# One more down-projection unit ahead of the next block's output projection, in a Hymba-style encoder layer on one core

## The chip, the core and the metric

The kernel runs on one core of a Trainium2 chip. The time is device microseconds of one execution, the median of three runs. The engines named here are TensorE (PE: matmuls and transposes, PEld its weight loads), VectorE (DVE), ScalarE (ACT), GpSimd (POOL) and SyncE (SP), whose queue issues the loads from and stores to device memory.

## The reference

One layer over 2048 tokens of width 1024, in float32, and then a final norm:

```python
h = rmsnorm(x, norm1_g)
proj = h @ w_in                       # q, k, v, z, xbc, dt
attn = rmsnorm(windowed_attention(q, k, v, sink, cos, sin), attn_out_g)
ssd = ssd_mixer(z, silu(dwconv(xbc)), dt, ...)   # two scans, gated, normed
mixed = concatenate([attn, ssd])
x = x + mixed @ w_out
h = rmsnorm(x, norm2_g)
u = dwconv(h @ w_up, ffn_conv_w, ffn_conv_b)     # 3 taps, 2 x 2816 columns
gate, val = split(u, 2)
x = x + (silu(gate) * val) @ w_down
return rmsnorm(x, final_norm_g)
```

## The kernel before

Activations lie with channels on the partitions. The 2048 tokens make four blocks of 512 (`NB`), and block `j` has `x1_j` (8 tiles of 128 channels by 512 tokens) as its residual stream, named `x` in the trace.

**Matmuls in three products.** Each float32 operand is split into a rounded high part and a low part. `mm3` (L105 to L108) makes hi times hi (L106), hi weight times lo activation (L107) and lo weight times hi activation (L108), all three into the same PSUM tile.

**Weights.** `wplan` lists every weight slice in the order of its use. `w_raw` loads a slice into `wraw` (L127, SP queue), `w_split` makes its high part `whi` on ScalarE (L141) and its low part `wlo` mostly on GpSimd (L142). `next_w` hands out the next slice and starts those behind it. `wraw`, `whi` and `wlo` have two buffers each, so slice n + 2 is cast when slice n is used up. A slice of `w_out` or `w_up` has 1024 columns (512 KB), one of `w_down` for a group of three pairs has 768 (384 KB).

**The feed-forward part of a block.** The 22 channel pairs (gate and value) come in six groups: 4, 4, 4, 4, 3, 3. For each pair `up_mm` makes two PSUM tiles of 24 matmuls and `up_unit` does convolution and gate (`fa`, `fth`) and writes `f` and its low part. `down_unit(j, g, cp)` adds group `g` to two tiles of `x1`: two PSUM tiles (`dn_b`), for a group of three pairs 9 matmuls each, and after each an update of `x` on VectorE (L1108). The units of group `g - 1` follow the up pairs of group `g`.

**The PSUM tiles** of up, `wo` and `dn` come from one pool, `psm`, with four buffers; each unit takes two.

**Between the blocks.** Beside block `j` run attention and scan of block `j + 1` (the `side` streams), which fill `mx`, named `mixed`. When they are done, `wo_split` scales `mx` and splits it into `m_hi` (ScalarE, L989) and `m_lo` (VectorE, L990), 8 tiles in two calls of 4. `wo_x1` loads the new residual `x1_{j+1}` (L996, 2 MB); `wo_unit` (four of them, 48 matmuls each) multiplies by `w_out`, adds to `x1_{j+1}` (L1029) and adds the square to `n_ss`. `h2_stage` has two steps. The first, `rstd_cols`, transposes the sum of squares on TensorE (`r_ps`), reduces it, and takes the power on GpSimd. The second, `rstd_bcast` and the loop behind it, transposes the result back (`r_pr`), copies it (`r`), and makes the 8 tiles `h2t` (L1040, VectorE) with `h_hi` (L207, ScalarE) and `h_lo` (L208, VectorE and GpSimd in turn). The first up pair of block `j + 1` reads them; for this pair the products go over the 8 tiles with both weights at each tile.

**Order.** The program order of a unit of work is that of the calls. The kernel is built with `tile.TileContext(nc, schedule_with_timeline_sim=True)`: a planner with modelled times sets the order on each engine, and may place a later instruction ahead of one that it takes to be waiting. Buffers of a pool are handed out by it too.

Of the kernel before, what the change touches and what calls it, by code (L numbers as in the profile page):

```python
# [28 lines left out]
GROUPS = [(0, 4), (4, 4), (8, 4), (12, 4), (16, 3), (19, 3)]  # L29
# [28 lines left out]
def block_kernel(ctx: ExitStack, tc: tile.TileContext, a: dict, out: bass.AP):  # L58
# [46 lines left out]
    def mm3(ps, whi, wlo, xhi, xlo, first, last):  # L105
        nc.tensor.matmul(ps, whi, xhi, start=first, stop=False)  # L106
        nc.tensor.matmul(ps, whi, xlo, start=False, stop=False)  # L107
        nc.tensor.matmul(ps, wlo, xhi, start=False, stop=last)  # L108
# [6 lines left out]
    wplan = [(a["w_ch"][c], 1024) for c in range(2)]  # L115
# [3 lines left out]
    def w_raw(i):  # L119
        if i >= len(wplan) or i in wraws:  # L120
            return
        src, m = wplan[i]
        raw = wpool.tile([P, 1024], F32, tag="wraw", name="wraw")
        dst = raw[:, :m]
        if len(src.shape) == 3:
            dst = dst.rearrange("p (i n) -> p i n", i=2)
        nc.sync.dma_start(dst, src)  # L127
        wraws[i] = raw

    def w_split(i):  # L130
        if i >= len(wplan) or i in wdone:
            return
        w_raw(i)
        m = wplan[i][1]
        raw = wraws[i]
        if i in wplace:
            hi, lo = wplace.pop(i)
        else:
            hi = wpool.tile([P, 1024], F32R, tag="whi", name="whi")
            lo = wpool.tile([P, 1024], F32R, tag="wlo", name="wlo")  # L140
        A.copy(hi[:, :m], raw[:, :m])  # L141
        (V if i < WV or i in WVS else G).tensor_tensor(lo[:, :m], raw[:, :m], hi[:, :m].bitcast(F32), ALU.subtract)  # L142
        wdone[i] = (hi, lo)

    def next_w():
        i = wpos[0]
        wpos[0] += 1
        w_split(i)
        w_raw(i + 1)
        w_split(i + 1)  # L150
        w_raw(i + 2)
        return wdone.pop(i)
# [35 lines left out]
    def new_ss(name):  # L188
        return [tpool.tile([P, FW], F32, tag="rstd", name=f"{name}_ss", bufs=1)]
# [98 lines left out]
    def flush():  # L288
        for f in pend:
            f()  # L290
        pend.clear()
# [25 lines left out]
    def new_mm(name):  # L317
        return [psm.tile([P, 512], F32, tag="mm", name=f"{name}_b{b}") for b in range(2)]
# [727 lines left out]
    def up_mm(j, pr, ws):  # L1046
        h2hi, h2lo = h2[j]
        ps = new_mm(f"up{j}_{pr}")
        if len(ws) > 2:
            ps += new_mm(f"up{j}_{pr + 1}")  # L1050
        order = [(i, k) for k in range(NK) for i in range(len(ws))]
        for i, k in order if pr == 0 else sorted(order):
            mm3(ps[i], ws[i][0][:, ksl(k)], ws[i][1][:, ksl(k)], h2hi[:, k], h2lo[:, k], k == 0, k == NK - 1)
        return ps
# [42 lines left out]
    def down_unit(j, g, cp, fs, w):  # L1097
        k0, nk = GROUPS[g]
        whi, wlo = w
        x1 = xone[j]  # L1100
        if j < NB - 1:
            ps = new_mm(f"dn{j}_{g}_{cp}")
            for i in range(2):
                for k in range(nk):
                    kk = ksl(i * nk + k)
                    mm3(ps[i], whi[:, kk], wlo[:, kk], fs[:, k, 0, :TB], fs[:, k, 1, :TB], k == 0, k == nk - 1)
                xv = x1[:, 2 * cp + i, 0:TB]
                V.tensor_tensor(xv, xv, ps[i], ALU.add)  # L1108
            return
        for i in range(2):  # L1110
            for b in range(2):
                down_part(j, g, 2 * cp + i, b, fs, w)
# [3 lines left out]
    def down_part(j, g, c, b, fs, w):  # L1116
        k0, nk = GROUPS[g]
        x1 = xone[j]
        n0, n1 = PART[b]
        pool, tag = (pss, "sc") if c % 2 == 0 else (psa, "ac")  # L1120
        ps = pool.tile([P, 512], F32, tag=tag, name=f"dn{j}_{g}_{c}_{b}")
        for k in range(nk):
            q = (c % 2) * nk + k
            mm3(
                ps[:, : n1 - n0], w[0][:, ksl(q)], w[1][:, ksl(q)],
                fs[:, k, 0, n0:n1], fs[:, k, 1, n0:n1], k == 0, k == nk - 1,
            )
        n1 = min(n1, TB + 1)
        V.tensor_tensor(x1[:, c, n0:n1], x1[:, c, n0:n1], ps[:, : n1 - n0], ALU.add)
# [82 lines left out]
    def w_wo():  # L1212
        return [(a["w_out"][c], 1024) for c in range(NK)]

    def w_dn(g):
        k0, nk = GROUPS[g]
        return [(a["w_dn"][cp][:, :, k0 * P : (k0 + nk) * P], 2 * nk * P) for cp in range(4)]
# [17 lines left out]
    for j in range(NB):  # L1235
        for g, (k0, nk) in enumerate(GROUPS):
            wplan += [(a["w_up"][k0 + i, q], 1024) for i in range(nk) for q in range(2)]
            if g > 0:
                wplan += w_dn(g - 1)
        if j + 1 < NB:  # L1240
            wplan[-2:-2] = w_wo()
        wplan += w_dn(len(GROUPS) - 1)

    def step(streams, n=1):
        for _ in range(n):
            for s in streams:
                next(s, None)

    def drain(s):
        for _ in s:  # L1250
            pass
# [105 lines left out]
    def start_side(j):  # L1357
        side.clear()
        due[:] = [0.0, 0.0]
        if j == NB:  # L1360
            return None
        m = new_mixed(j)
        side.extend([(chunks(attn, j, m), RATE[0]), (chunks(ssd, j, m), RATE[1])])
        return m

    def pace(n):
        for i, (s_, rate) in enumerate(side):
            due[i] += n * rate
            while due[i] >= 1:
                due[i] -= 1  # L1370
                next(s_, None)
# [12 lines left out]
    for j in range(NB):  # L1384
        more = j + 1 < NB
        if j > 0:
            mx = start_side(j + 1)
        fss = []
        for g, (k0, nk) in enumerate(GROUPS):
            fs = big.tile([P, SLOT], F32R, tag="big", name=f"f{j}_{g}").rearrange(  # L1390
                "p (k s n) -> p k s n", k=4, s=2
            )
            i = 0
            if j == 0 and g == 0 and UP2:
                wt = big.tile([P, SLOT], F32R, tag="big", name="wup")
                for q in range(2):
                    wplace[wpos[0] + 2 + q] = [wt[:, 1024 * (2 * q + z) : 1024 * (2 * q + z) + 1024] for z in range(2)]
                ps = up_mm(j, 0, [next_w() for _ in range(4)])
                for i in range(2):
                    if RPD == i:  # L1400
                        drain(rp)
                    up_unit(j, i, fs, i, ps[2 * i : 2 * i + 2])
                    pace(2)
                i = 2
            for i in range(i, nk):
                drain(rp)
                up_unit(j, k0 + i, fs, i, up_mm(j, k0 + i, [next_w(), next_w()]))
                step([fin], 2)
                pace(2)
            fss.append(fs)  # L1410
            if g == len(GROUPS) - 1:
                flush()
                for s_, _ in side:
                    drain(s_)
            if not more and g == len(GROUPS) - 1:
                wt = [big.tile([P, SLOT], F32R, tag="big", name=f"wdn{z}") for z in range(2)]
                for q in range(4):
                    wplace[len(wplan) - 4 + q] = [t[:, 768 * q : 768 * q + 768] for t in wt]
            if g > 0:
                for cp in range(4):  # L1420
                    if more and g == len(GROUPS) - 1 and cp == 2:
                        break
                    down_unit(j, g - 1, cp, fss[g - 1], next_w())
                    pace(1)
                    if more and g == len(GROUPS) - 1:
                        wo_split(j + 1, mx, 4 * cp, 4 * cp + 4)
        g = len(GROUPS) - 1
        if more:
            wo_x1(j + 1)
            ss = new_ss(f"n2_{j + 1}")  # L1430
            for cp in range(4):
                wo_unit(j + 1, cp, [next_w(), next_w()], ss)
            h2s = h2_stage(j + 1, ss)
            for cp in (2, 3):
                down_unit(j, g - 1, cp, fss[g - 1], next_w())
                step([h2s])
        else:
            last_down(g, fss[g])
            return
        for cp in range(4):  # L1440
            down_unit(j, g, cp, fss[g], next_w())
            step([h2s])
        fin = final(j)
# [79 lines left out]
```

## Time and profile before

| | |
|---|---|
| median of 3 runs | 2461.11 us |
| lowest, highest | 2459.13, 2463.56 us |
| profiled execution: its time | 2459.2 us |
| profiled execution: span from first to last instruction | 2457.1 us |
| busy TensorE, VectorE, ScalarE, GpSimd | 96%, 69%, 44%, 44% of the span |
| mean granted TensorE clock | 0.987 of full speed |

In a row of a timeline the first number is the start in us from the start of the span, the second the duration in us, then engine, line, operation, output and inputs with shapes. `x4` means that four like instructions are merged into the row. What stands in brackets is the idle time of that engine just before the row, and what ended it. Where a row says `<-DVE x L1108`, the instruction started when line 1108 on VectorE, which writes `x`, was done.

### The profile page before, as it was taken

Reading aid. Unit: us, or ns where it says so; the run is one execution under the profiler, and the core shown is the slowest. Engines: PE = TensorE matmul, PEld = TensorE weight load, DVE = VectorE, ACT = ScalarE, POOL = GpSimd, SP = SyncE. Lnnn points to the kernel's source line nnn. Section 1 sums busy time; section 2 is a strip of 40 time slices with the busy share of each in tenths; the row PEclk is TensorE's granted clock in tenths of the full one; section 3 lists DMA queues with packets and bytes.
Section 4 is the critical chain, followed back from the end, with each engine's and each line's share of the span. In section 5 each row is a group of like instructions: output and inputs, shape, how many; then the busy total and the mean of one; then the engine's idle time right before and its main releaser. Section 6 shows DMA issues by size and latency. Waiting matters only on the chain.

```text
span 2457.1 us, 31337 instructions
## 1 busy us (share of the span) xinstructions
PE 2347.2 (96%) x11440; PEld 1955.7 (80%) x11440; DVE 1687.5 (69%) x3056; ACT 1075.5 (44%) x1818; POOL 1086.0 (44%) x585
## 2 busy tenths in 40 slices
PE   8999999897999999999999999999999999999997
PEld 6878797776788878778787877787888877788887
DVE  5757777777886684569877675698776556844445
ACT  5444656345454443435443443354444333433334
POOL 1114314463644544455444454555444436544444
PEclk9999999998999999999999999999999999999999
DMA  6567445883444333334434333343342232333332
GB/s 229 166 194 221 134 148 181 253 274 115 130 129 126 117 125 101 124 93 152 123 117 128 122 112 116 92 153 118 114 129 90 86 121 85 121 103 95 95 92 80
DMA packets 172461, 325.82 MB, mean 133 GB/s; under 512 B 12690, under 2 KB 83730, under 8 KB 172308
## 3 DMA queue, kind: packets, MB, share of 16 engines
q1 hardware_dynamic: 172308, 323.83, 41.8%
q8 instruction: 90, 1.47, 0.2%
q14 instruction: 63, 0.52, 0.1%
HBM read 277.77 MB, written 44.71 MB: 131 GB/s over the span
## 4 chain that ended last, share of the span: by engine, by line
PE 45%; DVE 14%; POOL 2%; ACT 2%; issue 2%; DMA 1%; DVEq 0%; POOLq 0%; ACTq 0%
PE up_b L108 8%; PE up_b L107 8%; PE up_b L106 8%; DVE fa L1065 4%; PE dn_b L106 3%; PE dn_b L107 3%; PE dn_b L108 3%; PE dn L107 2%; PE dn L106 2%; PE dn L108 2%; PE wo_b L108 2%; PE wo_b L106 2%; PE wo_b L107 2%; POOL wlo L142 1%; DVE ab L893 1%
## 5 line engine op out<-in xcount | busy, mean ns | idle before, releaser
L142 POOL TENSOR_TENSOR wlo<-wraw,whi 128x1024 fp32r<-128x1024 f32 (+1 forms) x306 | 738.2, 2413 | 895.4 <-ACT whi L141 837.6
L108 PE MATMUL up_b<-h_hi,wlo 128*128 128x512 f32 x1392 | 551.7, 396 | 14.7 <-POOL wlo L142 14.7
L106 PE MATMUL up_b<-h_hi,whi 128*128 128x512 f32 x1392 | 551.3, 397 | 3.4 <-ACT whi L141 2.3
L107 PE MATMUL up_b<-h_lo,whi 128*128 128x512 f32 x1392 | 549.2, 395 | 1.9 <-DVE h_lo L208 1.9
L141 ACT CAST whi<-wraw 128x1024 fp32r<-128x1024 f32 (+1 forms) x330 | 338.9, 1027 | 467.6 <-PE up_b L107 120.9
L1065 DVE SCALAR_TENSOR_TENSOR fa<-up_b,fcw,fa 128x511 f32<-128x511 f32 (+2 forms) x396 | 271.7, 687 | 211.2 <-ACT fa L1067 206.7
L108 PEld LDWEIGHTS up_b<-h_hi,wlo 128*128 128x128 f32 x1392 | 262.4, 189 | 77.7 <-POOL wlo L142 21.1
L106 PEld LDWEIGHTS up_b<-h_hi,whi 128*128 128x128 f32 x1392 | 261.9, 188 | 62.7 <-ACT whi L141 4.9
L107 PEld LDWEIGHTS up_b<-h_lo,whi 128*128 128x128 f32 x1392 | 262.1, 188 | 60.0 <-DVE h_lo L208 3.4
L106 PE MATMUL dn_b<-f,whi 128*128 128x512 f32 x528 | 211.4, 400 | 0.4 <-DVE x L1108 0.2
L107 PE MATMUL dn_b<-f,whi 128*128 128x512 f32 x528 | 208.7, 395 | 0.0
L108 PE MATMUL dn_b<-f,wlo 128*128 128x512 f32 x528 | 204.2, 397 | 0.0
L1092 ACT CAST f<-fth 128x512 fp32r<-128x512 f32 (+1 forms) x88 | 54.6, 620 | 216.5 <-DVE fth L1089 175.5
L1087 ACT ACTIVATE fth<-fa 128x512 f32<-128x512 f32 (+1 forms) x88 | 55.6, 632 | 212.6 <-DVE fa L1065 167.6
L1108 DVE TENSOR_TENSOR x<-x,dn_b 128x512 f32<-128x512 f32 x144 | 97.6, 681 | 59.9 <-PE dn_b L108 59.6
L1067 ACT ACTIVATE fa<-up_b,fcw 128x512 f32<-128x512 f32 x176 | 135.9, 773 | 0.2
L106 PEld LDWEIGHTS dn_b<-f,whi 128*128 128x128 f32 x528 | 99.8, 189 | 22.9 <-DVE x L1108 1.1
L108 PEld LDWEIGHTS dn_b<-f,wlo 128*128 128x128 f32 x528 | 99.3, 188 | 22.5 <-POOL wlo L142 0.2
L107 PEld LDWEIGHTS dn_b<-f,whi 128*128 128x128 f32 x528 | 99.2, 188 | 21.0
L893 DVE SCALAR_TENSOR_TENSOR ab<-ab,ldt,mask 128x128 f32<-128x128 f32 x256 | 95.3, 442 | 21.8 <-DMA ab<-acs_d 21.8
L1065 DVE SCALAR_TENSOR_TENSOR fa<-hal,fcw,fa 128x2 f32<-128x2 f32 (+1 forms) x264 | 101.0, 383 | 4.6
L1093 DVE TENSOR_TENSOR f<-fth,f 128x512 fp32r<-128x512 f32 (+1 forms) x88 | 78.9, 897 | 30.9 <-ACT f L1092 30.1
(333 smaller groups left out, 4880.4 us busy)
## 6 DMA issues: line engine op xcount, KB each, us to landing
wraw<-in_w_up SPq DMA_DIRECT2D x176, 512.0 KB
wraw<-in_w_dn SPq DMA_DIRECT2D x64, 512.0 KB
wraw<-in_w_out SPq DMA_DIRECT2D x36, 512.0 KB
ab<-acs_d SPq DMA_DIRECT2D x32, 512.0 KB
wraw<-in_w_ch SPq DMA_DIRECT2D x28, 512.0 KB
wraw<-in_w_dn SPq DMA_DIRECT2D x32, 384.0 KB
ak<-ks_d SPq DMA_DIRECT2D x14, 768.0 KB
xt<-in_x SPq DMA_DIRECT2D x16, 512.0 KB
```

The lines of the kernel that those rows point to most:

```text
L106: nc.tensor.matmul(ps, whi, xhi, start=first, stop=False)
L107: nc.tensor.matmul(ps, whi, xlo, start=False, stop=False)
L108: nc.tensor.matmul(ps, wlo, xhi, start=False, stop=last)
L141: A.copy(hi[:, :m], raw[:, :m])
L142: (V if i < WV or i in WVS else G).tensor_tensor(lo[:, :m], raw[:, :m], hi[:, :m].bitcast(F32), ALU.subtract)
L893: (G if i < SUBP[0 if first else 1] else V).scalar_tensor_tensor(ab[:, i, d], ab[:, i, d], ldt[:, d, c, h : h + 1], mask3[:, 2 * d * P : ( ...
L1065: V.scalar_tensor_tensor(o, src, w(q), o, ALU.mult, ALU.add)
L1067: A.activation(ai[:, 0:TB], u, AF.Identity, bias=w(3), scale=w(2))
L1087: A.activation(th[:, :n], acc[:, 0, :n], AF.Tanh)
L1092: A.copy(fs[:, idx, 0, :n], th[:, :n])
L1093: V.tensor_tensor(fs[:, idx, 1, :n], th[:, :n], fs[:, idx, 0, :n].bitcast(F32), ALU.subtract)
L1108: V.tensor_tensor(xv, xv, ps[i], ALU.add)
```

## The change

Group 4 is the last but one. Its four down units stood two ahead of the next block's output projection and two behind it; now three stand ahead and one behind. The weight order follows: the eight slices of `w_out` go in ahead of the last slice of group 4 in place of the last two. The two calls of `wo_split` stay behind the first and the second unit. Behind the output projection the first step of `h2_stage` now comes at once, then the last unit of group 4, then the second step. The last block is as it was.

```diff
         if j + 1 < NB:
-            wplan[-2:-2] = w_wo()
+            wplan[-1:-1] = w_wo()
         wplan += w_dn(len(GROUPS) - 1)
...
                 for cp in range(4):
-                    if more and g == len(GROUPS) - 1 and cp == 2:
+                    if more and g == len(GROUPS) - 1 and cp == 3:
                         break
                     down_unit(j, g - 1, cp, fss[g - 1], next_w())
                     pace(1)
-                    if more and g == len(GROUPS) - 1:
+                    if more and g == len(GROUPS) - 1 and cp < 2:
                         wo_split(j + 1, mx, 4 * cp, 4 * cp + 4)
...
             h2s = h2_stage(j + 1, ss)
-            for cp in (2, 3):
-                down_unit(j, g - 1, cp, fss[g - 1], next_w())
-                step([h2s])
+            step([h2s])
+            down_unit(j, g - 1, 3, fss[g - 1], next_w())
+            step([h2s])
```

## Rows read from the trace of the kernel before

**Rows 1.** The page: the span and the busy time of the engines.

```profile
span 2457.1 us, 31337 instructions
...
PE 2347.2 (96%) x11440; PEld 1955.7 (80%) x11440; DVE 1687.5 (69%) x3056; ACT 1075.5 (44%) x1818; POOL 1086.0 (44%) x585
```

**Rows 2.** Timeline of TensorE at the entries of the three hand-overs.

```profile
1016.78 0.50 PE L106 MATMUL wo_b<-m_hi,whi 128*128 128x512 f32 x1 [0.49 <-ACT whi L141]
...
1034.92 0.50 PE L108 MATMUL wo_b<-m_hi,wlo 128*128 128x512 f32 x1 [0.97 <-POOL wlo L142]
...
1495.31 0.39 PE L106 MATMUL dn_b<-f,whi 128*128 128x512 f32 x1
...
1503.58 0.39 PE L106 MATMUL wo_b<-m_hi,whi 128*128 128x512 f32 x1
...
1509.42 0.76 PE L106 MATMUL wo_b<-m_hi,whi 128*128 128x512 f32 x1 [5.21 <-DVE x L1108]
...
1992.07 0.77 PE L106 MATMUL wo_b<-m_hi,whi 128*128 128x512 f32 x1 [5.18 <-DVE x L1108]
```

**Rows 3.** Windows after long waits: stretch, length, TensorE busy (matmuls), granted clock, DMA share, GB/s.

```profile
1509.42:1513.78 4.36, 4.36 (x10) 0.51 0.60 179
1992.07:1995.11 3.04, 3.04 (x7) 0.52 0.46 77
2066.93:2070.32 3.39, 3.39 (x8) 0.53 0.53 155
```

**Rows 4.** Timeline of VectorE at the entry of the second hand-over.

```profile
1499.83 0.74 DVE L990 SCALAR_TENSOR_TENSOR m_lo<-mixed,gv,m_hi 128x512 fp32r<-128x512 f32 x1
...
1503.73 4.94 DVE L990 SCALAR_TENSOR_TENSOR m_lo<-mixed,gv,m_hi 128x512 fp32r<-128x512 f32 x2
1508.60 0.68 DVE L1108 TENSOR_TENSOR x<-x,dn_b 128x512 f32<-128x512 f32 x1
...
1509.99 0.68 DVE L1108 TENSOR_TENSOR x<-x,dn_b 128x512 f32<-128x512 f32 x1
...
1518.03 0.69 DVE L1029 TENSOR_TENSOR x<-x,wo_b 128x512 f32<-128x512 f32 x1 [5.07 <-DMA x<-in_xT]
```

**Rows 5.** Timeline of ScalarE and of GpSimd, same entry.

```profile
1501.65 1.04 ACT L141 CAST whi<-wraw 128x1024 fp32r<-128x1024 f32 x1
1503.60 1.05 ACT L141 CAST whi<-wraw 128x1024 fp32r<-128x1024 f32 x1 [0.91 <-PE dn_b L107]
...
1496.24 1.85 POOL L142 TENSOR_TENSOR wlo<-wraw,whi 128x768 fp32r<-128x768 f32 x1 [3.70 <-ACT whi L141]
1502.77 5.36 POOL L142 TENSOR_TENSOR wlo<-wraw,whi 128x1024 fp32r<-128x1024 f32 x2 [4.67 <-ACT whi L141]
```

**Rows 6.** Windows, last `wo` matmul to the up pair's end, three hand-overs; columns as Rows 3.

```profile
1062.30:1103.57 41.27, 38.87 (x170) 1.00 0.31 97
1555.38:1596.67 41.29, 39.05 (x170) 1.00 0.32 96
2037.40:2079.20 41.80, 39.02 (x166) 0.96 0.28 83
```

**Rows 7.** Timeline of TensorE at the exits of the first and third hand-over.

```profile
1067.35 0.60 PE L165 MATMUL r_ps<-ident,n_ss 128*128 128x128 f32 x4
...
1074.49 0.60 PE L183 MATMUL r_pr<-ident,r_c 128*128 128x128 f32 x4
...
1098.37 0.50 PE L108 MATMUL up_b<-h_hi,wlo 128*128 128x512 f32 x1 [1.37 <-POOL wlo L142]
...
2066.93 0.79 PE L108 MATMUL up_b<-h_hi,wlo 128*128 128x512 f32 x1 [2.77 <-POOL wlo L142]
```

**Rows 8.** Timeline of GpSimd at the exits of the first and third hand-over.

```profile
1094.36 1.63 POOL L208 TENSOR_TENSOR h_lo<-h2t,h_hi 128x512 fp32r<-128x512 f32 x1 [1.95 <-ACT h_hi L207]
1095.95 4.73 POOL L142 TENSOR_TENSOR wlo<-wraw,whi 128x1024 fp32r<-128x1024 f32 x2
...
2068.15 1.31 POOL L208 TENSOR_TENSOR h_lo<-h2t,h_hi 128x512 fp32r<-128x512 f32 x1 [1.28 <-ACT h_hi L207]
```

## Prediction

> **What bounds the kernel now.** I read the page first: TensorE is busy for 96% of the span [rows 1], so only what makes TensorE stand still or run slowly can move the time. Then I read TensorE's timeline at the three places that the diff touches, the hand-overs between token blocks (0 to 1, 1 to 2, 2 to 3; below the first, second and third), for its idle times and what ended them. Each hand-over has two weak places.
>
> *The entry*, where the output projection `wo` starts. In the second and third hand-over TensorE issues two `wo` matmuls and then stands for 5.21 and 5.18 us until an `x` update of L1108 is done [rows 2]. The matmuls after that run at half clock: 10 take 4.36 us and 7 take 3.04 us at a granted 0.51 and 0.52, near 1.2 of 2.4 GHz [rows 3], where 36 `dn_b` matmuls between 1495.31 and 1503.58 took 8.27 us [rows 2], 0.23 each. So half clock costs 4.36 - 10 x 0.23 = 2.05 and 3.04 - 7 x 0.23 = 1.42 us. The first hand-over loses only 0.49 and 0.97 us [rows 2].
>
> Why 5.2 us: L1108 is queued on VectorE behind two `m_lo` that took 4.94 us together, and those ran while GpSimd did two `wlo` in one stretch of 5.36 us, 1502.77 to 1508.13 [rows 4, 5]. One `m_lo` alone takes 0.74 [rows 4], so two would need some 1.4 us. The matmul that waits needs one of the four `psm` buffers, and these come free only by VectorE's reads: the next two L1108 end at 1509.28 and 1510.67 [rows 4].
>
> *The exit*, from the last `wo` matmul to the end of the next block's first up pair, takes 41.27, 41.29 and 41.80 us, with 2.2 to 2.8 us of idle TensorE in each [rows 6]. Here `h2` must be made: sum of squares, transposes, power, eight normalised tiles with two splits each. In the first hand-over the last low part of `h2` is done by GpSimd at 1095.99, 33.7 us after the last `wo` matmul, and a `wlo` of an up weight is queued right behind it, which TensorE meets at 1098.37 with 1.37 us of waiting [rows 7, 8]. In the third it is done at 2069.46, 32.1 us after, and the first `wlo` costs 2.77 us and then half clock (3.39 us for 8 matmuls, 1.55 too much) [rows 3, 7, 8]. So behind `wo` TensorE has too little work already, and in front of `wo` it has too little in two hand-overs of three.
>
> **The change, part by part.** No instruction is added or removed. Per hand-over, one `down_unit` of group 4 (3 pairs x 3 products x 2 tiles = 18 matmuls, two L1108, one weight slice with its load, cast and `wlo`) goes from behind `wo` to ahead of it. 18 matmuls are 18 x 0.23 = 4.14 us.
>
> *Entry, the weight.* The weight order is now dn, dn, dn, then `w_out`. The cast that stood at 1501.65 is for a slice of 768 columns and its `wlo` 1.85 us long like the one at 1496.24 [rows 5] instead of 2.4 like those of the `w_up` weights [rows 8]; the unit's third matmul needs it at about 1504.0 and it is there at about 1504.5: 0.5 us of waiting. The first `w_out` slice takes the place of the second, cast at 1503.60 [rows 5], ready near 1507.5, before `wo` starts.
>
> *Entry, the buffers.* The moved unit takes two `psm` buffers. The first is free early. In the second and third hand-over the other is the very one that the third `wo` matmul waits for now. TensorE asks for it at 1503.58 + 0.5 + 2.1 = 1506.2. On VectorE the first `m_lo` now passes at 1504.5, the shorter `wlo` ending, but if GpSimd takes the next `wlo` before the second `m_lo` starts, that one passes at 1507.5 and L1108 ends near 1508.8: a wait of 2.6 us. If VectorE comes first, L1108 ends at 1506.5 and the wait is 0.3. I take 2.6, since in the row the two `m_lo` took turns with the two `wlo` [rows 4, 5]. It is close to the 2.77 us behind which half clock is seen, so I add the third hand-over's 1.4 for it; the other bound is 0.
>
> The Trainium skill (SBUF — State Buffer, Who interferes with whom) states that a VectorE instruction with two SBUF inputs contends with a GpSimd instruction that reads SBUF, and that the issue order decides who blocks. The trace agrees with the first part: L990 reads two SBUF tiles and stretches to 4.94 us for two [rows 4]. The second part leaves open which of my two waits comes.
>
> *Entry, the sum.* First: +4.14 - 1.46 + 0.5 (weight) + 0.5 (`wo`'s own buffer, whose L1108 is late by the same `m_lo`; now its third matmul waits for a cast alone [rows 2]) = +3.7. Second: +4.14 - 5.21 - 2.05 + 0.5 + 2.6 + 1.4 = +1.4. Third: +4.14 - 5.18 - 1.42 + 0.5 + 2.6 + 1.4 = +2.0. Together +7.1 at the last `wo` matmul. With the early L1108 and no half clock the second and third fall to -2.3 and -1.7, together -0.3 with the first.
>
> *Entry, the queues.* On SP the load of `x1` waits for the last `m_lo` as before; the weight load that is now ahead of it is one of 384 KB in place of 512. The first `wo` update waits for that load until 1518.03 [rows 4], but TensorE has four buffers and doesn't wait; with `wo` starting 1.5 us later this cover grows. I cost it at nothing; if the cover goes, the price is about the 0.97 us that the first hand-over pays now.
>
> *Exit.* Behind `wo` there are 90 `dn_b` matmuls instead of 108, so TensorE reaches the up projection 4.14 us earlier. What it meets there is `h2`. Engine order here is not program order: the transposes of the sum stand 5.05 us or 22 matmuls behind `wo`, those of the power 12.19 us or 51 matmuls [rows 6, 7], where the code puts them 18 and 36 behind. A planner with modelled times placed them, so I expect them at the same distance again, with the next down matmuls in between; TensorE then doesn't stall at the now adjacent `step([h2s])`. Casts and `wlo` also keep their times, one weight further on in the list. So `h2` keeps its 33.7 (third: 32.1) us, and the up pair ends 3 + 24 matmuls (6.2 us) behind that, plus half clock after the thin stretch, for which I take 0.8 between 0 and 1.55. First and second: 33.7 + 6.2 + 0.8 = 40.7, that is -0.6 each; third: 32.1 + 6.2 + 0.8 = 39.1, -2.7. Together -3.9. Bounds: all 4.14 saved each time (-12.4), or nothing (0).
>
> The sum is +7.1 - 3.9 = +3.2 us. The profiled execution took 2459.2 us (span 2457.1), the median of the three runs is 2461.11; the sum on the median is 2464.3, and I say 2464.
>
> **The rivals.** 0.2% of the time, about what a measurement of this kernel can tell from no change, is 4.9 us: faster begins under 2456.2, slower above 2466.0.
>
> *The entry stall is filled* (chance 0.20). VectorE gets its turn before the second `wlo`, L1108 is there, TensorE never stands long enough to lose its clock: entry -0.3. With an exit of -1.2, -1.2 and -3.6 (no half clock) the sum is -6.3, 2454.8. For it: the `wlo` beside the `m_lo` is shorter. Against it: GpSimd has its next `wlo` ready within some 0.3 us. It decides if L1108 ends before about 1507 in the second hand-over's terms.
>
> *The exit gives nothing back* (0.28). The second up weight's `wlo` is ready 4 us earlier against `h2` and goes ahead of the last low parts on GpSimd, which push `h2` out by some 2 us; or first and second up tile advance in step and hold both weight buffers to the end, so that the next pair waits for a cast and a `wlo`. Either eats the 3.9 us: +7.1, 2468.2. For it: GpSimd's queue there is already the last link [rows 8]. Against it: 2.2 us of idle TensorE that earlier weights could fill.
>
> *The move isn't seen* (0.08). The planner may put `wo` matmuls into the moved unit's wait for its buffer, and the order is then near to the old one: 0, 2461.1.
>
> **How the numbers follow.** The forecast, a wash with a small loss, gets 0.44 and a range of its own of 2457 to 2466. Same is 0.44 + 0.08 = 0.52, slower 0.28, faster 0.20. For 8 in 10 I go from 2455, which takes in most of the filled entry, to 2470.
>
> **What the profile after would show.** Right: 54 `dn_b` matmuls ahead of `wo`; in the second and third hand-over a wait of some 2.6 us inside the third unit, ended by L1108, in place of 5.2 behind it; the transposes again 22 and 51 matmuls behind `wo`; the last low part of `h2` 32 to 34 us behind it, and more TensorE idle time in the first up pair. Wrong: entry without a wait over 1 us, or an exit of under 38 us (then it is faster), or an exit over 41 us, or TensorE waiting at the transposes (slower).

## The result, and the profile after

The changed kernel takes 2492.31 us in the median of 4 runs (2490.24 to 2497.75), the kernel before 2462.34 us beside it (2459.13 to 2464.98): a ratio of 1.0123, 95% interval 1.0104 to 1.0142. It is slower by 30 us, and by far outside the predicted range.

The profiled execution is the slowest of the four, 2497.75 us. Its page and TensorE's timeline at the places of [rows 1, 2, 7]:

```profile
span 2496.0 us, 31332 instructions
...
PE 2371.4 (95%) x11440; PEld 1970.3 (79%) x11440; DVE 1702.1 (68%) x3056; ACT 1076.9 (43%) x1818; POOL 1082.4 (43%) x585
```

```profile
1025.19 0.47 PE L106 MATMUL wo_b<-m_hi,whi 128*128 128x512 f32 x1 [0.57 <-DVE x L1108]
1038.60 0.50 PE L108 MATMUL wo_b<-m_hi,wlo 128*128 128x512 f32 x1 [1.61 <-POOL wlo L142]
...
1515.92 0.39 PE L106 MATMUL dn_b<-f,whi 128*128 128x512 f32 x1
...
1525.51 0.50 PE L108 MATMUL dn_b<-f,wlo 128*128 128x512 f32 x1 [0.69 <-POOL wlo L142]
1529.45 0.50 PE L106 MATMUL dn_b<-f,whi 128*128 128x512 f32 x1 [2.05 <-DVE x L1108]
...
1582.19 0.60 PE L165 MATMUL r_ps<-ident,n_ss 128*128 128x128 f32 x4
...
1589.39 0.60 PE L183 MATMUL r_pr<-ident,r_c 128*128 128x128 f32 x4
...
1632.23 0.44 PE L753 MATMUL sc<-ak,aq 128*128 128x384 f32 x1 [2.42 <-DVE mxs L755]
1651.38 1.11 PE L781 MATMUL pt<-ident,sm 128*128 128x128 f32 x4 [4.41 <-DVE pl L785]
...
1712.58 0.77 PE L811 MATMUL aps<-one,ass 128*128 128x128 f32 x2 [2.81 <-DVE ass L808]
```

**The hand-overs did about what was forecast.** Both waits in the moved unit are there, 0.69 and 2.05 us. The transposes stand 5 and 12 us behind the last `wo` matmul (1577.14), as in [rows 7]. The exits, to be held against [rows 6], are the first three lines of these windows (stretch, length, TensorE busy, granted clock, DMA share, GB/s):

```profile
1071.70:1110.32 38.62, 35.32 (x151) 0.96 0.26 79
1577.14:1615.82 38.68, 35.52 (x151) 0.96 0.26 80
2074.40:2115.25 40.85, 36.68 (x148) 0.92 0.24 71
1529.45:1533.50 4.05, 4.05 (x18) 1.00 0.45 145
2026.18:2029.50 3.32, 3.32 (x8) 0.50 0.43 103
...
1651.38:1655.50 4.12, 4.12 (x12) 0.50 0.31 114
1712.58:1716.70 4.12, 3.54 (x9) 0.50 0.11 17
1615.82:2012.65 396.83, 383.63 (x1741) 0.98 0.36 111
```

From the first `dn` matmul to the first up pair's end the three hand-overs take 98.8, 99.9 and 102.6 us, against 96.2, 101.4 and 101.2 before: +2.5 us together, where +3.2 was forecast.

**The loss lies behind the hand-overs**, in a part that the forecast didn't look at: the body of a block, from the end of its first up pair to the next hand-over. Body 1 takes 405.6 us in place of 391.7 (+13.9), body 2 396.8 in place of 381.3 (+15.5), the last +2.9. Some 4 us more are ahead of the first hand-over (it starts at 1011.5 in place of 1007.4), where both kernels have the same instructions; over the runs below that start lies between 1001 and 1013. These pieces add up to the 38.9 us between the two profiled spans, of the slowest execution after and the fastest before; the medians are 30 apart. Body 2 before, in the same columns as the last line above:

```profile
1596.67:1977.96 381.29, 375.77 (x1742) 1.00 0.37 115
```

The same matmuls were busy for 7.9 us more, at a clock of 0.98 in place of 1.00, and TensorE stood idle for 13.2 us in place of 5.5. That is the 15.5. Of the idle time, 9.6 us are three waits for VectorE, the last three lines of the timeline (2.42, 4.41, 2.81 us), of which body 2 of the kernel before has the first two at 0.63 and 0.47 us and the third not at all; behind two of them the windows show half clock, 1.2 GHz, for 4 us. All three lie in the first 100 us of the body, and body 1 has the same three. They belong to the attention: its scores `sc` with their maxima `mxs`, the transposed softmax rows `pt` with their low part `pl`, and the sums `ass` of its norm.

**What VectorE does there.** Attention for the next block starts beside the first up pair. L776 multiplies its softmax rows, four instructions for each half chunk. VectorE and then GpSimd in the changed kernel:

```profile
1524.35 4.45 DVE L990 SCALAR_TENSOR_TENSOR m_lo<-mixed,gv,m_hi 128x512 fp32r<-128x512 f32 x2
...
1616.38 0.62 DVE L755 CUSTOM_DVE_ANT_0 sm<-sc,mask,vecs 128x384 f32<-128x384 f32 x1 [5.57 <-PE sc L754]
1624.66 5.32 DVE L776 TENSOR_SCALAR sm<-sm,rsm 128x384 f32<-128x384 f32 x3
1642.36 5.62 DVE L776 TENSOR_SCALAR sm<-sm,rsm 128x384 f32<-128x384 f32 x4
1647.90 2.82 DVE L1093 TENSOR_TENSOR f<-fth,f 128x512 fp32r<-128x512 f32 x1
1650.65 0.68 DVE L785 TENSOR_TENSOR pl<-pt,ph 128x512 fp32r<-128x512 f32 x1
```

```profile
1624.09 3.18 POOL L204 TENSOR_TENSOR n_ss<-n_ss,n_sq 128x512 f32<-128x512 f32 x2 [2.86 <-ACT n_sq L202]
1627.23 2.53 POOL L142 TENSOR_TENSOR wlo<-wraw,whi 128x1024 fp32r<-128x1024 f32 x1
1629.72 1.38 POOL L204 TENSOR_TENSOR n_ss<-n_ss,n_sq 128x512 f32<-128x512 f32 x1
...
1642.52 1.42 POOL L204 TENSOR_TENSOR n_ss<-n_ss,n_sq 128x512 f32<-128x512 f32 x1 [1.55 <-ACT n_sq L202]
1643.92 2.49 POOL L142 TENSOR_TENSOR wlo<-wraw,whi 128x1024 fp32r<-128x1024 f32 x1
1646.37 1.40 POOL L204 TENSOR_TENSOR n_ss<-n_ss,n_sq 128x512 f32<-128x512 f32 x1
```

And the same two engines before, VectorE first:

```profile
1603.48 1.41 DVE L776 TENSOR_SCALAR sm<-sm,rsm 128x384 f32<-128x384 f32 x4
1620.61 1.41 DVE L776 TENSOR_SCALAR sm<-sm,rsm 128x384 f32<-128x384 f32 x4
```

```profile
1600.34 1.30 POOL L204 TENSOR_TENSOR n_ss<-n_ss,n_sq 128x512 f32<-128x512 f32 x1
1604.84 2.93 POOL L142 TENSOR_TENSOR wlo<-wraw,whi 128x1024 fp32r<-128x1024 f32 x1 [3.19 <-ACT whi L141]
...
1617.48 2.86 POOL L142 TENSOR_TENSOR wlo<-wraw,whi 128x1024 fp32r<-128x1024 f32 x1
1622.90 2.40 POOL L142 TENSOR_TENSOR wlo<-wraw,whi 128x1024 fp32r<-128x1024 f32 x1 [2.56 <-ACT whi L141]
```

Before, the four scalings stood in GpSimd's gaps (1601.64 to 1604.84, 1620.34 to 1622.90) and took 1.41 us. Now GpSimd has its sums of squares for the final norm and its low parts back to back there, and four scalings take 5.62 us. Behind them come the 2.82 us of L1093 and the `pl` for which TensorE waits until 1651.38.

The four can be taken apart. In these rows each takes in two neighbours, the first and second, second and third, third and fourth:

```profile
1642.36 1.80 DVE L776 TENSOR_SCALAR sm<-sm,rsm 128x384 f32<-128x384 f32 x2
1642.69 3.94 DVE L776 TENSOR_SCALAR sm<-sm,rsm 128x384 f32<-128x384 f32 x2
1644.08 3.90 DVE L776 TENSOR_SCALAR sm<-sm,rsm 128x384 f32<-128x384 f32 x2
```

So the second ends at 1644.16, the third at 1646.63, the fourth at 1647.98, and the three GpSimd rows beside them at 1643.94, 1646.41 and 1647.77: each scaling ends 0.2 us behind one GpSimd instruction. In the two whole traces 23 scalings of 96 are long like this after and 11 before; every one ends 0.21 to 0.23 us behind the end of a GpSimd instruction, and none that began while GpSimd was in one was short. While GpSimd has one instruction behind the other, one scaling gets through for each.

**What put them there.** The order on TensorE in the first up pair of blocks 1 and 2, gate tile G and value tile V, with the number of matmuls in a row (the trace names no buffers, but the lines L106, L107 and L108 of the 48 matmuls come in this order):

```
before   G22 V2 G2 V22
after    G13 V2 G3 V14 G2 V2 G3 V3 G1 V1 G2 V2
```

Before, the gate tile was done 22 matmuls (5 us) ahead of the value tile. Now the second weight is ready earlier against `h2`, and I take it that the planner therefore lets both tiles go on in step; what it weighed no trace shows. The order does come with the change: with the first or the third hand-over changed alone (below), it stands in that one only. In block 2 both tiles end together, at 1615.82, and so do the two weight buffers; ScalarE waited for them:

```profile
1615.32 1.05 ACT L141 CAST whi<-wraw 128x1024 fp32r<-128x1024 f32 x1 [5.11 <-PE up_b L107]
```

VectorE was idle for 5.57 us at the same time (row 1616.38 above). So the first theory: the in-step pair shifts VectorE's work by some 5 us against GpSimd's.

### The profile page after: what moved, and what is told of

It reads as the page before. It is cut to its first block, busy times and chain, and to the rows that moved or that the text cites. A ratio compares the mean times of both kernels' runs of the same rounds, so it can differ in the third digit from the quotient of the medians.

```text
span 2496.0 us, 31332 instructions
## 1 busy us (share of the span) xinstructions
PE 2371.4 (95%) x11440; PEld 1970.3 (79%) x11440; DVE 1702.1 (68%) x3056; ACT 1076.9 (43%) x1818; POOL 1082.4 (43%) x585
## 4 chain that ended last, share of the span: by engine, by line
PE 48%; DVE 13%; DMA 2%; POOL 1%; ACT 1%; issue 1%; DVEq 0%; SPq 0%; ACTq 0%; POOLq 0%
PE up_b L108 8%; PE up_b L107 8%; PE up_b L106 8%; PE dn_b L106 3%; PE dn_b L107 3%; PE dn_b L108 3%; DVE fa L1065 3%; PE dn L107 2%; PE dn L106 2%; PE dn L108 2%; PE wo_b L108 2%; DVE sm L776 1%; PE wo_b L107 1%; PE wo_b L106 1%; POOL wlo L142 1%
## 5 line engine op out<-in xcount | busy, mean ns | idle before, releaser
L107 PE MATMUL up_b<-h_lo,whi 128*128 128x512 f32 x1392 | 556.1, 400 | 10.3 <-DVE h_lo L208 6.5
L108 PE MATMUL up_b<-h_hi,wlo 128*128 128x512 f32 x1392 | 557.8, 401 | 6.7 <-POOL wlo L142 6.3
L106 PE MATMUL up_b<-h_hi,whi 128*128 128x512 f32 x1392 | 557.6, 402 | 5.7 <-ACT whi L141 2.7
L1065 DVE SCALAR_TENSOR_TENSOR fa<-up_b,fcw,fa 128x510 f32<-128x510 f32 (+2 forms) x396 | 271.1, 686 | 210.8 <-ACT fa L1067 206.7
L108 PEld LDWEIGHTS up_b<-h_hi,wlo 128*128 128x128 f32 x1392 | 266.4, 191 | 71.5 <-POOL wlo L142 13.0
L107 PEld LDWEIGHTS up_b<-h_lo,whi 128*128 128x128 f32 x1392 | 265.7, 191 | 71.8 <-DVE h_lo L208 8.7
L106 PEld LDWEIGHTS up_b<-h_hi,whi 128*128 128x128 f32 x1392 | 266.1, 191 | 67.5 <-ACT whi L141 5.7
L106 PE MATMUL dn_b<-f,whi 128*128 128x512 f32 x528 | 212.0, 402 | 4.1 <-DVE x L1108 4.1
L107 PE MATMUL dn_b<-f,whi 128*128 128x512 f32 x528 | 209.3, 396 | 0.0
L108 PE MATMUL dn_b<-f,wlo 128*128 128x512 f32 x528 | 204.9, 398 | 1.6 <-POOL wlo L142 1.6
L106 PEld LDWEIGHTS dn_b<-f,whi 128*128 128x128 f32 x528 | 100.1, 190 | 25.9 <-DVE x L1108 5.0
L108 PEld LDWEIGHTS dn_b<-f,wlo 128*128 128x128 f32 x528 | 99.7, 189 | 25.4 <-POOL wlo L142 3.1
L107 PEld LDWEIGHTS dn_b<-f,whi 128*128 128x128 f32 x528 | 99.7, 189 | 21.1
L1093 DVE TENSOR_TENSOR f<-fth,f 128x512 fp32r<-128x512 f32 (+1 forms) x88 | 78.8, 895 | 28.6 <-ACT f L1092 28.1
L106 PE MATMUL pj_b<-h_hi,whi 128*128 128x512 f32 x208 | 86.3, 416 | 12.1 <-ACT h_hi L235 7.0
```

The lines of the kernel that those rows point to most:

```text
L1065: V.scalar_tensor_tensor(o, src, w(q), o, ALU.mult, ALU.add)
L1093: V.tensor_tensor(fs[:, idx, 1, :n], th[:, :n], fs[:, idx, 0, :n].bitcast(F32), ALU.subtract)
```

## Experiments

Ratios are to the kernel before, run beside each.

**Which hand-over.** The changed order in the first hand-over alone, and in the third alone:

```diff
-            wplan[-1:-1] = w_wo()
+            w_at = 1 if j == 0 else 2        # third alone: j == 2
+            wplan[-w_at:-w_at] = w_wo()
...
+        ahead = 3 if j == 0 else 2           # third alone: j == 2
...
-                    if more and g == len(GROUPS) - 1 and cp == 3:
+                    if more and g == len(GROUPS) - 1 and cp == ahead:
...
```

The cut at the end is the order behind `wo`, the changed one or the old one to match.

> Three units ahead only in the first hand-over, two and two in the second and third. If the loss is made per hand-over, in the block behind it: 2.6 us in the hand-over and some 14 in block 1, so 2475 to 2481 us. Rival (the loss builds up, each hand-over's shift making the next worse): not over 2470 us.

> Three units ahead only in the third hand-over, two and two in the first and second. The last block has no attention and scan beside it. If the collision partner is the first attention chunk: +1 us in the hand-over and some 3 in the last block, so 2460 to 2468 us. Rival (the partner is the final norm of the block before, which runs beside the last block too): 2472 us or more.

First alone: 2479.1 us, 1.0079 [1.0060, 1.0097]. Third alone: 2462.04 us, 1.0009 [0.9996, 1.0021]. Both as expected. With the first alone, body 1 takes 404.8 us and body 2 381.3, as before the change. The hand-over with no attention behind it, in the last block, costs no more than can be told (its profile has 3 us more in the last body). The second alone wasn't run; with the 15.5 us of body 2 above, the loss is made in each body that has attention beside it.

**The in-step pair by itself.** The kernel before, with the first pair's 48 matmuls chained in the order of the loop, three for G, three for V (`one(i, k)` is the `mm3` of tile `i` at `h2` tile `k`):

```diff
...
-        for i, k in order if pr == 0 else sorted(order):
+        if pr == 0 and j > 0:
+            one(0, 0)
+            for i, k in order[1:]:
+                with tc.issue_after(nc.cur_bb.bb.instructions[-1]):
+                    one(i, k)
+            return ps
+        for i, k in order if pr == 0 else sorted(order):
```

> The kernel before, with two down units ahead of the output projection, but in blocks 1 to 3 the first up pair's two tiles are forced to advance in step on TensorE (at each of the 8 tiles of h2 first the gate tile's three matmuls, then the value tile's). In-step theory: the moved unit isn't needed for the loss, so 2480 to 2495 us with the same three waits in blocks 1 and 2. Rival (the moment of the start decides): 2458 to 2468 us.

2510.84 us, 1.0211 [1.0195, 1.0226]: with no unit moved, more than the whole loss, and above the range I gave. Its waits, over bodies 1 and 2 (us in total, times, longest), take in the three of the changed kernel, to 0.1 us:

```profile
PE pt L781 <- DVE pl L785: 9.0, 2, 4.5
PE aps L811 <- DVE ass L808: 5.4, 2, 2.7
...
PE sc L753 <- DVE mxs L755: 4.9, 2, 2.5
```

Not all of it is the same loss. Of the 52.8 us between the profiled spans, 21.7 lie in the hand-overs, where the change costs 2.5. In the strict order the value tile's first matmul waits inside the pair for the cast of its weight, here in the second hand-over:

```profile
1612.91 0.79 PE L106 MATMUL up_b<-h_hi,whi 128*128 128x512 f32 x1 [4.53 <-ACT whi L141]
```

The bodies take 14.9, 12.2 and 2.9 us more than before, against 13.9, 15.5 and 2.9 with the change.

**The change without the in-step pair.** The value tile's matmuls queued behind the gate tile's:

```diff
...
+        if pr == 0 and j > 0:
+            for k in range(NK):
+                one(0, k)
+            with tc.issue_after(nc.cur_bb.bb.instructions[-1]):
+                for k in range(NK):
+                    one(1, k)
+            return ps
```

> The changed kernel, but in blocks 1 to 3 the 24 matmuls of the first up pair's value tile are queued behind the 24 of its gate tile on TensorE, as they stand in the kernel before. In-step theory (the loss comes from the first up pair's two tiles advancing together, so that both finish late, both weight buffers stay taken, and VectorE gets the whole convolution at once on top of the first attention chunk): the waits of 2.4, 4.4 and 2.8 us in the first groups of blocks 1 and 2 go, what is left is the hand-overs' own some 2 to 8 us, so 2464 to 2471 us. Rival (the first up pair simply starts at another moment against attention and the final norm, and the planner's order for them collides whatever the order inside the pair): 2485 us or more.

2475.74 us, 1.0071 [1.0056, 1.0086]: between what the two theories said. The pair's order is a sufficient cause, but half of the loss is left without it. In body 2 the eight scalings still average 949 ns: in each group of four the last one still meets a `wlo` and takes 2.5 to 2.6 us, the other three 0.42. Bodies 1 and 2 take 5.9 and 6.0 us more than before, and the hand-overs, which without the in-step pair give back less at their exits, together 6.5.

**Attention later.** Nothing of attention and scan beside the first two pairs of group 0, one step more with each pair of group 2; on the changed kernel, on the one before, and on the one with the gate tile first:

```diff
                 step([fin], 2)
-                pace(2)
+                if j == 0 or g != 0 or i > 1:
+                    pace(3 if j > 0 and g == 2 else 2)
```

> The changed kernel, with the attention and scan of the next block started two up pairs later (nothing of them beside the first two pairs of group 0, one step more with each of the four pairs of group 2). If the loss comes from the next block's attention being queued on VectorE just when both tiles of the first pair come out together, so that VectorE falls behind and TensorE waits for it three times, it falls to under half: 2462 to 2475 us. If it comes from the weight buffers that the in-step pair holds (late casts and low parts), which this edit leaves as it is, the time stays above 2485.

> The kernel before with the same later start of attention and scan: what this edit is worth where the first pair runs one tile after the other. If VectorE is the bound in the first 100 us of a block there too (95% busy), 2455 to 2461; if the later start only moves the load, 2459 to 2464; if the later end of attention delays the output projection, over 2466.

> The changed kernel with both: the value tile queued behind the gate tile in the first pair, and attention two pairs later. If the two causes add up (the first alone gave 2475.7), this comes to the forecast's 2462 to 2466; if what the first left over is something else in the hand-over, 2470 to 2476.

2487.55 us, 1.0115 [1.0095, 1.0135]; 2480.85 us, 1.0080 [1.0063, 1.0098]; 2481.46 us, 1.0085 [1.0068, 1.0101]. The first lies where the rival put it, and yet doesn't speak for the rival: the edit alone costs 0.8% on the kernel before, over the 2466 us of its worst case, and the third is out of both its ranges. The scalings show what I had missed. They meet GpSimd at the new place too, 872 ns in the mean with the changed kernel and with the one before, 871 with the gate tile first. What can be read is the difference: with the edit in both, the change costs 6.7 us in place of 30, and with the gate tile first 0.6. It depends on what attention meets.

**The norm later.** The block's final norm (sums on ScalarE and GpSimd, scaling L1201 on VectorE) from the third up pair on; on the changed kernel, the one before, and the one with the gate tile first:

```diff
-                step([fin], 2)
+                if j == 0 or g != 0 or i > 1:
+                    step([fin], 2)
                 pace(2)
```

> The changed kernel, with the final norm of the block before started with the third up pair of group 0 instead of the first. If GpSimd's part of this norm (n_ss and n_sq, which stand beside VectorE's slow scalings of the softmax) is what turns the in-step pair into a loss, the loss of about 30 us falls to under half: 2462 to 2475 us. If the loss is VectorE's idle time at the end of the pair and more work than it can catch up, with the norm only a part of it, the time falls by less than 10 us: 2482 to 2492. If the norm has no part in it: 2490 to 2495.

> The kernel before with the final norm of the block before started at the third up pair of group 0, as in the run that took half of the loss off the changed kernel. If VectorE with its neighbour GpSimd is too full in the first 100 us of a block there too, a little faster than before: 2452 to 2459 us. If the norm only stands in the way where the pair ran in step, no difference: 2459 to 2464. If the later norm delays something of its own, over 2466.

> The changed kernel with the value tile queued behind the gate tile in the first pair and the norm later. If the two runs' gains (about 15 us each) are of separate causes, this comes to the forecast's 2460 to 2467; if they are one and the same (room on VectorE at the head of the body), about 2472 to 2477.

2477.36 us, 1.0061 [1.0039, 1.0083]; 2463.05 us, 1.0004 [0.9995, 1.0013]; 2470.24 us, 1.0032 [1.0019, 1.0044]. The first and third fall between the ranges of their theories. Half of the loss goes, nothing is gained on the kernel before, and with the gate tile first three quarters go. But this edit moves a GpSimd part and a VectorE part at once.

**One part of the norm left out**, on the changed kernel: the sums, or the scaling.

```diff
             # sums left out
-            add_sq(ss, x1[:, k, 0:n], k, n, G, f"n3_{j}")
+            if k == 0:
+                add_sq(ss, x1[:, k, 0:n], k, n, G, f"n3_{j}")
...
             # scaling left out
-            V.scalar_tensor_tensor(
+            if k == 0:
+                V.scalar_tensor_tensor(
...
```

> The changed kernel with the sum of squares of the block's final norm taken over its first of eight tiles alone: it leaves out seven ScalarE squares and seven GpSimd additions per block and keeps all of VectorE's work. If the price is VectorE's instructions stretched beside GpSimd, the loss of about 30 us falls by 8 us or more: under 2484. If it is VectorE's amount of work alone, no change: 2487 to 2495.

> The changed kernel with VectorE's final scaling done for the first of eight tiles alone: it leaves out seven VectorE instructions of about 1 us per block and keeps GpSimd's additions. If the price is VectorE's amount of work, the loss falls by 10 us or more (7.6 us of work per block): under 2482. If the price is the stretched softmax scalings, which stand earlier beside GpSimd's additions, little change: 2485 to 2495.

Without the sums 2463.34 us, 1.0021 [1.0010, 1.0033]; without the scaling 2485.18 us, 1.0112 [1.0095, 1.0129]. Both as the theory of the stretched scalings expected, the second at the edge of its range. GpSimd's sums out of the way take away nearly all of the loss, though the pair is still in step and VectorE has all of its work. Two things came together there: the scalings also came later (the first 18.5 us behind the pair's end, 7.9 in the changed kernel), and the kernel before without its sums wasn't run.

Seven instructions of about 1 us less for VectorE in each body take off some 4 us in all (26.1 us are left beside the kernel before, of 30.0). This run says little of the first two waits: in the changed kernel these instructions stand behind them.

```profile
1665.69 6.86 DVE L1201 SCALAR_TENSOR_TENSOR x<-x,gv,r 128x512 f32<-128x512 f32 x7 [0.20 <-ACT r L185]
```

So they bear on the third wait alone. That one is gone without them in both bodies, while the second is longer, 6.0 us each:

```profile
PE pt L781 <- DVE pl L785: 12.0, 2, 6.0
...
PE sc L753 <- DVE mxs L755: 6.1, 4, 2.4
```

The first two waits have the stretched scalings ahead of them; the third, for `ass`, needs the norm's scaling as well.

L776 in the head of body 2 (busy time, mean ns), changed kernel, without sums, without scaling:

```profile
L776 DVE TENSOR_SCALAR sm<-sm,rsm 128x384 f32<-128x384 f32 x8 | 11.4, 1469 | 0.1
```

```profile
L776 DVE TENSOR_SCALAR sm<-sm,rsm 128x384 f32<-128x384 f32 x8 | 2.9, 410 | 0.0
```

```profile
L776 DVE TENSOR_SCALAR sm<-sm,rsm 128x384 f32<-128x384 f32 x8 | 11.3, 1468 | 0.1
```

**The scaling on ScalarE**, on the changed kernel, the one before, the one with the gate tile first, and the one with the norm later:

```diff
-                if mx is None and ENG[2] == "A":
+                if mx is not None or ENG[2] == "A":
                     A.activation(x, x, AF.Copy, scale=rs[kv][:, i : i + 1])
```

> The changed kernel with the scaling of the softmax (four instructions for each half chunk beside the block bodies) on ScalarE in place of VectorE. If VectorE's scalings, stretched from 0.35 to 1.8 us each beside GpSimd, are what TensorE's waits rest on, most of the loss goes: 2462 to 2472 us. If the loss is VectorE's lateness as a whole (idle while the pair ran, and no room to catch up), some of it goes: 2472 to 2485. If VectorE is not the engine: 2488 to 2495, or more, since ScalarE gets longer.

> The kernel before with the same scaling on ScalarE: what that edit is worth without the change. 2452 to 2462 us if VectorE bounds the head of the body there too; 2462 to 2470 if ScalarE's own chain (cast, square, exp) gets longer for it.

> The changed kernel with the softmax scaling on ScalarE and the value tile queued behind the gate tile. If the in-step pair costs only through those scalings, this is where the scaling alone came out: 2463 to 2468. If the pair has a price of its own besides (late casts), 2456 to 2462, which would be the forecast's hand-over gains without its costs.

> The changed kernel with the softmax scaling on ScalarE and the final norm later. If both edits take away the same stretched scalings, no more is to be had: 2463 to 2468. If VectorE is still too full at the head of the body, 2455 to 2462, and this version would be no slower than the kernel before.

2466.39 us, 1.0023 [1.0014, 1.0033]; 2461.89 us, 1.0002 [0.9991, 1.0013]; 2463.08 us, 1.0016 [1.0003, 1.0028]; 2470.05 us, 1.0050 [1.0032, 1.0068]. The edit is worth nothing before the change and 1% after it, with the pair in step as it was, and the gate tile first adds nothing that can be told. The last of the four is a miss: with the norm later besides, it is slower than the scaling on ScalarE alone, the intervals just touching. Its waits show 8.2 us for `wlo` and 6.1 for `pl` over bodies 1 and 2, against 1.9 and 2.7 with the scaling alone; why stays open. No version with the moved unit is faster than the kernel before.

**The scalings in one view.** The mean of the eight scalings in the head of body 2, from the view of lines, beside the ratio, for the kernels that have them on VectorE:

| mean ns | kernels (ratio) |
|---|---|
| 410 to 418 | before (1), before with norm later (1.0004), third hand-over alone (1.0009), no sums (1.0021), gate first and norm later (1.0032) |
| 871 to 872 | attention later: before (1.0080), gate first (1.0085), changed (1.0115) |
| 949 to 952 | norm later (1.0061), gate first (1.0071) |
| 1468 to 1469 | no scaling (1.0112), changed (1.0123), before in step (1.0211) |

In the kernel with the first hand-over alone (1.0079) it is 1465 in body 1 and 417 in body 2. The later attention apart, which moves more than this, the ratio rises with the mean.

## Why the prediction was wrong

**The entry** was right in kind: +5.2, +1.2 and +2.3 us, where +3.7, +1.4 and +2.0 stood. In the second and third the 2.05 us wait is there for the reason given: two `m_lo` took turns with two `wlo` for 4.45 us (row 1524.35), with GpSimd first. The half clock allowed for came in the third (0.50) and not in the second (1.00). In the first, the account took off both old waits, 1.46 us, but the one for `wlo` is still there and grew from 0.97 to 1.61 us (row 1038.60).

**The exit** gave back 2.7, 2.6 and 1.0 us, where 0.6, 0.6 and 2.7 stood. The steps of `h2` kept their distances, as said; in the second hand-over its last low part is

```profile
1609.76 1.30 POOL L208 TENSOR_TENSOR h_lo<-h2t,h_hi 128x512 fp32r<-128x512 f32 x1 [1.95 <-ACT h_hi L207]
```

and ends 33.9 us behind `wo`. What was mis-sized is the rest: 3 + 24 matmuls and some half clock, 7.0 us, stood behind it, and 4.9, 4.8 and 8.3 us were measured. With both tiles in step only 21 and 20 matmuls were left in the first two. Together entry and exit are +2.5 against +3.2, and that is partly luck: the entry came out 1.6 us dearer and the exit 2.3 us cheaper. With the scalings on ScalarE in both kernels the change costs 4.5 us, near to what the account gave.

**The step that failed** is the end of the account. The sum stopped at the first up pair's end, and took the rest of the block as the same. It is in the second rival that both tiles may go on in step and hold both weight buffers, but priced there at no more than what the exit would have given back, with "the next pair waits for a cast and a `wlo`" as the harm. That was the wrong harm. What comes behind that pair is VectorE's fullest stretch (busy for 42.7 and 45.3 us of 50 in the two stretches from 1590 on in the kernel before), with GpSimd's norm and low parts beside it, and there a shift of 5 us sets which of the two finds the other in its way. The price is 13.9 and 15.5 us in the two bodies. Every sign that I had named for being right is in the trace, the transposes to one matmul, and none of those for being wrong: all of them stood in the hand-overs, so they couldn't show this.

**The rivals.** A filled entry stall and an unseen move are out: the waits and the 54 `dn` matmuls ahead of `wo` are in the trace. The second rival named the right event, with +7.1 us in place of 30, and the wrong way round at the exit, where the in-step pair gave back more, not less. The exits of the first rival, by the account's own terms, would be -1.4, -1.4 and -3.5; nothing hangs on the difference.

**Shown and only argued.** Shown: the loss of some 15 us a body needs attention beside the body (third hand-over alone); the in-step order alone brings all three waits; the long scalings end with GpSimd's instructions; the loss goes down to 4.5 us with the scalings on ScalarE, an edit that is worth nothing on the kernel before. That it isn't VectorE's amount of work rests on the run without the sums, which kept all of it. Not shown: why the planner gave the in-step order; how much of the gain without the sums is the sums (seven ScalarE squares went too, and the scalings moved); how much of the third wait is the scalings' and how much the norm's; and why the two edits of the last run get in each other's way.

## What to carry to other kernels

An account of a moved step can't end where the move ends: follow it to the next stretch in which two engines are full beside each other, and ask what happens there if one arrives 5 us later. Where a planner sets the order, look first at the order it now gives, before any duration. And small instructions that stand in another engine's gap are a debt: moving the four scalings to ScalarE gained nothing by itself, but with it the same shift cost 0.2% in place of 1.2%.

## What the runs showed of the hardware

Four scalings of 128x384 took 1.41 us in GpSimd's gap and 5.62 us beside its back-to-back additions and subtractions, with each GpSimd instruction at close to its usual time: 2.49 us for a `wlo` against 2.40. VectorE bore nearly all of it, since each long scaling ended 0.22 us behind the end of a GpSimd instruction (34 of 34 in the two traces). The Trainium skill (SBUF — State Buffer, Who interferes with whom) counts `tensor_scalar` among the VectorE operations that can take the ports shared with GpSimd, and says that the one that issues second blocks fully. The ends in the trace agree with that; which ports were used no run here shows.

Two like stretches had different clocks behind them. In the second and third hand-over TensorE stood 0.69 and 0.66 us, then ran seven matmuls, then stood 2.05 us both times. Behind it one window shows 18 matmuls at 1.00, the other 8 at 0.50.
